# One plain feed-forward group instead of two, with the weight sums of gate and up on VectorE

## The chip, the cores and the metric

The kernel runs on one core of a Trainium2 chip. The metric is the device time of one launch in microseconds (us), the median of three runs. Engines are named as in the profile: PE is TensorE, which multiplies matrices (PEld is its weight load), DVE is VectorE, ACT is ScalarE, POOL is GpSimd, SP is SyncE, which issues nearly all DMAs.

## The reference

A decoder trunk of two layers over 1024 tokens of width 1024, in float32. Each layer mixes the tokens in four ways and adds the result to `x`; then comes the feed-forward part, which this change is about:

```python
D_FF = -(-8 * D_MODEL // (3 * 256)) * 256     # 2816
for l in range(DEPTH):                        # 2
    h = rmsnorm(x, attn_norm[l])
    proj = h @ w_in[l]
    ...                                       # latent attention, gated convolution, pooling, window attention
    x = x + mixed @ w_o[l]
    h2 = rmsnorm(x, ffn_norm[l])
    gate, up = jnp.split(h2 @ w_gate_up[l], 2, axis=-1)
    x = x + (jax.nn.silu(gate) * up) @ w_down[l]
return rmsnorm(x, final_norm)
```

## The kernel before

Activations lie with the features on the 128 partitions and the tokens along the row, in two halves of 512 tokens (`HALVES`). To keep float32 accuracy, each operand of a product is split into a high and a low part of type float32r: ScalarE casts (L283 or, with a gain, L286), VectorE subtracts (L284, L287). `mm3` (L272) then takes three matmuls for each pair of blocks: high x high, high x low, low x high.

The feed-forward's 2816 columns are worked through in 22 groups of 128 (`NFF`). A group computes gate and up for both halves of the tokens. There are two ways to do it. A *plain* group (`plain`, the first `NPL` = 2 groups of a layer) takes the weights as they are: for each half, gate and up are two products each (`product`) of four blocks, so eight products of 12 matmuls in all. Every other group treats gate/up and the two halves as a 2 x 2 matrix product in the Strassen-Winograd form, with seven products of 12 matmuls in place of eight. For that it needs sums and differences of both operands:

- of the activations, once a layer: `combine(j)` for j = 0 to 3 makes the blocks `hb[N1]`, `hb[N2]`, `hb[T3]`, `hb[T4]` from `hb[B11]`, `hb[B12]`, `hb[B21]`, `hb[B22]`, which `out_last` writes; VectorE and ScalarE do it (L1063, L1050, L1069, L1071 and the splits);
- of the weights, for each group: `GateUp.sums` (L1132 to L1134) and `GateUp.sum4` (L1154), four additions of 128x512 on GpSimd; `split1` to `split4` split the results;
- of the outputs: the products are added up in PSUM, where a copy by ScalarE (`snap`, L1176) and an addition by VectorE take intermediate values (L1188, L1502, L1514).

`gu_start` does a group's first two products, those with B11 and B21, which need no combined activations. `silu` (L1310) applies the activation on ScalarE and multiplies by the norm `r2` on GpSimd (L1312). `out_last` also adds up the squares for that norm (`ss2`, L324); `norm(u)` ends it. `combos(g)` makes, for each pair of groups, the same sums of the activations for the down projection and stores them to `ad`. The down projection has weight sums of its own: `dn_sums` loads blocks of `w_down`, adds them up on GpSimd in four operations of 128x256 (L161) and stores them to `qd`; the loop over the groups drives it with `next(sums)`, one block per group.

PSUM has eight banks of 128x512 in four tags (mm 2, s 3, t 2, pv 1); the tags of the seven-product groups rotate by the table `turns`. On-chip buffers are 47 slots of two halves, taken and returned first in, first out (`N_U`, `Slots`).

The order in which instructions are issued is not the written one. `order_engines` collects all instructions of the program, gives each group of instructions a place (its rank in the written order plus a shift from the table `MOVES`, by number of the group), and `arrange` simulates the engines with the costs in `length`; the ready instruction with the lowest place goes first. The order found is fixed with dependencies.

Of the kernel before, what the change touches and what calls it, by code (L numbers as in the profile page):

```python
# [25 lines left out]
NFF = DFF // P  # L26
# [15 lines left out]
NPL = 2  # L42
# [69 lines left out]
def trunk_kernel(ctx: ExitStack, tc: tile.TileContext, ins, out):  # L112
# [274 lines left out]
    for l in range(L):  # L387
# [731 lines left out]
        class GateUp:  # L1119
# [8 lines left out]
            def sums(self):  # L1128
                w1, w2 = self.raw
                q = self.q = F.pair()  # L1130
                a11, a22, a21 = F.ap(w1), F.ap(w1 + 1), F.ap(w2 + 1)
                pool.tensor_tensor(out=F.ap(q + 1), in0=a21, in1=a22, op=ALU.add)  # L1132
                pool.tensor_tensor(out=F.ap(q), in0=a21, in1=a11, op=ALU.add)
                pool.tensor_tensor(out=a21, in0=F.ap(q + 1), in1=a11, op=ALU.add)  # L1134
# [17 lines left out]
            def sum4(self):  # L1152
                q4 = F.ap(self.raw[1])
                pool.tensor_tensor(out=q4, in0=q4, in1=F.ap(self.raw[1] + 1), op=ALU.add)  # L1154
# [24 lines left out]
        def gu_start(w, between=None):  # L1179

            w.pa, pd = ps("aa"), ps("ad")
            product(w.pa, blocks(w.s1, 0), hb[B11])
            k1 = snap(w.pa)
            if between:
                between()
            product(pd, blocks(w.s2, 0), hb[B21])
            w.gate = tmp("tp")
            dve.tensor_tensor(out=w.gate, in0=pd, in1=k1, op=ALU.add)  # L1188
# [55 lines left out]
        for n in range(2):  # L1244
            R.free(kb_[1][n][1])
            R.free(va[2 + n][1])
        ma1 = norm_a(1)
        mix_values(*prev)
        for n in range(2):
            R.free(kb_[1][n][0])  # L1250
            R.free(va[n][1])
        ma0 = norm_a(0)
        out_some(len(parts))
# [3 lines left out]
        std = [GateUp(f) for f in range(2)]  # L1257
        std[0].split_plain()
# [4 lines left out]
        std[1].split_plain()  # L1263
# [4 lines left out]
        def plain(f, u):  # L1268

            w, b = std[f], ((B11, B21), (B12, B22))[u]  # L1270
            pg, pu = ps("wide"), ps("wide")
# [37 lines left out]
        def silu(g, r):  # L1309
            nonlocal last_silu  # L1310
            last_silu = act.activation(g, g, AF.Silu)  # L1311
            pool.tensor_tensor(out=g, in0=g, in1=r, op=ALU.mult)  # L1312
# [113 lines left out]
        w = GateUp(2)  # L1426
        plain(0, 0)
        combine(0)
        plain(1, 0)
        norm(0)  # L1430
        combine(1)
        plain_gates()
        plain(0, 1)
        norm(1)
        plain_silus()
        plain_gates()
        w.sums()
        combine(2)
        plain_acts()
        w.split1()  # L1440
        plain(1, 1)
        plain_silus()
        plain_gates()
        combine(3)
        w.split2()
        plain_acts()
# [3 lines left out]
        wn = GateUp(3)  # L1450
        w.split3()
        plain_silus()
        w.sum4()
        w.split4()
        plain_acts()
        for f in range(NPL, NFF):
            if wn:
                wn.sums()
            wnn = GateUp(f + 2) if f + 2 < NFF else None
            end = f == NFF - 1  # L1460
            gu_start(w, lambda: pending and second(*pending))
# [11 lines left out]
            if wn:  # L1473
# [5 lines left out]
            for i in w.s2:  # L1479
                R.free_pair(i)  # L1480
            k2 = snap(w.pa)
            if wn:
# [37 lines left out]
            neg_mul(F.ap(acts[f][0]), w.pa, gate)  # L1520
            if wn:
# [137 lines left out]
class Step:  # L1659
    __slots__ = ("ins", "eng", "rank", "before", "after", "tiles", "left", "ns", "tail", "ready", "sums", "bank", "onchip", "size", "start", "end", "table", "rows", "place")  # L1660

    def __init__(self, eng, rank):
# [4 lines left out]
        self.onchip = 0.0  # L1667
# [40 lines left out]
def length(eng, kind, i, ins, outs):  # L1708
    n = max(width(a) for a in ins + outs)
    ps = any(a.bass_ap.tensor.name.startswith("ps_") for a in ins)  # L1710
    if eng == "POOL":
        return 206 if kind == "InstMemset" else 1150 + 0.5 * n
# [19 lines left out]
def steps_of(tc):  # L1732
    steps, seen = [], {}
    table, runs = None, {"Silu": [], "Exp": []}
    for i in tc.nc.cur_bb.bb.instructions:
# [31 lines left out]
        else:  # L1767
            v.ns = length(eng, kind, i, ins, outs)
            if not any(a.bass_ap.tensor.name.startswith("ps_") for a in ins + outs):
                v.onchip = 0.7 if kind == "InstTensorScalarPtr" and len(ins) < 3 else 0.4  # L1770
# [39 lines left out]
def arrange(steps, rank=lambda v: v.rank):  # L1810
    queue, uses, freed, parked = {}, {}, {}, {}
# [21 lines left out]
    wire, pool_busy, last_fp32, table = 0.0, [], False, "Exp"  # L1833
# [5 lines left out]
    def takes(v, t):  # L1839
        for name in (x for x in v.tiles if x not in live):  # L1840
            tag = name.rsplit("_", 1)[0]
            if queue[tag][0] != name or not freed[tag] or freed[tag][0] + 40 > t:
# [3 lines left out]
    while any(now.values()) or any(later.values()):  # L1846
# [23 lines left out]
        for name in (x for x in v.tiles if x not in live):  # L1870
            tag = name.rsplit("_", 1)[0]
            if queue[tag][0] != name or not freed[tag]:
# [9 lines left out]
        for name in [x for x in v.tiles if x not in live]:  # L1882
            tag = name.rsplit("_", 1)[0]
            live.add(name)
            queue[tag].popleft()
            heapq.heappop(freed[tag])
# [17 lines left out]
        else:  # L1904
# [5 lines left out]
            if e == "DVE" and v.onchip:  # L1910
                ns += v.onchip * sum(max(0.0, min(b, t + ns) - max(a, t)) for a, b in pool_busy[-8:])
# [5 lines left out]
            if e == "POOL":  # L1917
                pool_busy.append((t, v.end))
# [6 lines left out]
        for name in v.tiles:  # L1925
            todo[name] -= 1
# [221 lines left out]
```

## Time and profile before

| | |
|---|---|
| median of 3 runs | 2062.74 us (2061.73 to 2062.99) |
| the profiled execution | 2061.72 us |
| its span, first to last instruction | 2059.9 us |
| granted TensorE clock | 0.998 |
| busy: PE, DVE, ACT, POOL | 2033.0, 1553.8, 979.5, 596.9 us |
| matmuls | 9418 |

In layer 0 `out_last` runs from about 366 us, the feed-forward's groups from about 388 to 820 us, the down projection to about 1040 us; layer 1 follows about 1010 us later. Busy times count every instruction from its start to its end, and instructions of one engine overlap at their edges, so a stretch can be all busy and still not be at the engine's best pace. In the timeline a row's first number is the start, the second the time from the first start to the last end of the merged instructions, and brackets hold the idle time before and what ended it.

### The profile page before, as it was taken

How to read it: one execution, taken by the hardware profiler on the slowest of the kernel's cores; microseconds unless marked ns; L12 is line 12 of the kernel's file. 1: busy time of each engine (PE TensorE's matmuls, PEld its weight loads, DVE VectorE, ACT ScalarE, POOL GpSimd, SP SyncE). 2: the span in 40 equal slices, each digit the busy share in tenths (PEclk: the TensorE clock that was granted, in tenths of full speed). 3: DMA queues.
4: the chain of work that ended last, by engine and by line, in shares of the span. 5: the costliest groups of instructions: out<-in, count | busy, mean ns of one | idle time of the engine just before them, and what ended most of it. 6: DMA issues, size and time to landing. Idle time of an engine off the chain costs nothing.

```text
span 2059.9 us, 26292 instructions
## 1 busy us (share of the span) xinstructions
PE 2033.0 (99%) x9418; PEld 1676.4 (81%) x9418; DVE 1553.8 (75%) x2430; ACT 979.5 (48%) x1722; POOL 596.9 (29%) x461
## 2 busy tenths in 40 slices
PE   8999999999999999999999999999999999999997
PEld 7887888878888888888888878878778888888887
DVE  7879988987776768655657898879877677686555
ACT  7447666653333334444443576666433333355332
POOL 0000000058776765100000000001787677640000
PEclk9999999999999999999999999999999999999999
DMA  5010222334444437866401102142444444498652
GB/s 181 34 58 24 79 88 86 138 121 168 170 156 167 166 138 257 313 221 204 152 33 44 47 21 91 64 144 81 160 168 163 153 166 153 145 333 278 197 177 86
DMA packets 148819, 289.76 MB, mean 141 GB/s; under 512 B 12608, under 2 KB 72000, under 8 KB 148688
## 3 DMA queue, kind: packets, MB, share of 16 engines
q1 hardware_dynamic: 148656, 288.03, 40.2%
q8 instruction: 74, 1.21, 0.2%
q14 instruction: 57, 0.47, 0.1%
q0 software_dynamic: 32, 0.04, 0.0%
HBM read 204.66 MB, written 83.36 MB: 140 GB/s over the span
## 4 chain that ended last, share of the span: by engine, by line
PE 89%; DVE 7%; DMA 1%; issue 1%; ACT 1%; POOL 1%; SPq 0%; DVEq 0%; ACTq 0%
PE ps_mm L272 35%; PE ps_s L272 26%; PE ps_t L272 10%; PE ps_pv L272 8%; DVE u L284 2%; PE ps_pv L962 2%; PE ps_t L950 1%; DVE u L287 1%; PE ps_s L896 1%; DVE u L324 1%; PE ps_t L336 1%; PE ps_s L898 1%; PE ps_s L897 1%; PE ps_pv L572 1%; DVE u L1099 1%
## 5 line engine op out<-in xcount | busy, mean ns | idle before, releaser
L272 PE MATMUL ps_mm<-u,u 128*128 128x512 f32 (+1 forms) x3394 | 848.8, 388 | 9.9 <-ACT u L286 7.1
L272 PEld LDWEIGHTS ps_mm<-u,u 128*128 128x128 f32 x3394 | 622.8, 188 | 136.2 <-ACT u L286 7.1
L272 PE MATMUL ps_s<-u,u 128*128 128x512 f32 x2648 | 649.4, 390 | 4.7 <-DVE u L284 3.6
L272 PEld LDWEIGHTS ps_s<-u,u 128*128 128x128 f32 x2648 | 496.8, 188 | 110.1 <-DVE u L284 4.4
L284 DVE TENSOR_TENSOR u<-u,u 128x1024 fp32r<-128x1024 f32 (+2 forms) x384 | 463.9, 1230 | 148.8 <-ACT u L283 129.3
L283 ACT CAST u<-u 128x1024 fp32r<-128x1024 f32 (+2 forms) x384 | 332.9, 888 | 464.9 <-PE ps_mm L272 178.4
L272 PE MATMUL ps_t<-u,u 128*128 128x512 f32 (+1 forms) x1146 | 274.4, 378 | 0.4 <-ACT u L283 0.4
L959 POOL MEMSET u<- 128x128 f32 x32 | 6.6, 230 | 847.8 <-PE ps_mm L272 637.8
L272 PEld LDWEIGHTS ps_t<-u,u 128*128 128x128 f32 x1146 | 206.3, 188 | 41.3 <-ACT u L283 0.8
L161 POOL TENSOR_TENSOR u<-u 128x256 f32<-128x256 f32 x176 | 196.8, 1118 | 73.2 <-DMA u<-in_w_dn 62.3
L1312 POOL TENSOR_TENSOR tp<-tp,u 128x512 f32<-128x512 f32 x88 | 147.1, 1672 | 209.6 <-ACT tp L1311 209.5
L272 PE MATMUL ps_pv<-u,u 128*128 128x512 f32 x744 | 184.7, 389 | 0.0
L272 PEld LDWEIGHTS ps_pv<-u,u 128*128 128x128 f32 x744 | 139.7, 188 | 29.0
L1311 ACT ACTIVATE tp<-tp 128x512 f32<-128x512 f32 x88 | 55.6, 632 | 134.1 <-DVE tp L348 133.4
L1132 POOL TENSOR_TENSOR u<-u,u 128x512 f32<-128x512 f32 x40 | 70.6, 1765 | 128.7 <-PE ps_s L272 55.5
L283 ACT CAST u<-ps_t 128x512 fp32r<-128x512 f32 (+4 forms) x136 | 64.8, 506 | 63.2 <-PE ps_t L950 38.9
L286 ACT ACTIVATE u<-u,par 128x512 fp32r<-128x512 f32 x100 | 69.3, 717 | 53.6 <-DVE u L1099 19.5
L284 DVE TENSOR_TENSOR u<-ps_t,u 128x512 fp32r<-128x512 f32 (+4 forms) x136 | 76.5, 583 | 17.8 <-ACT u L283 16.7
L287 DVE SCALAR_TENSOR_TENSOR u<-u,par,u 128x512 fp32r<-128x512 f32 x100 | 73.5, 757 | 7.5 <-ACT u L286 7.2
L348 DVE TENSOR_TENSOR tp<-tp,u 128x512 f32<-128x512 f32 x80 | 74.9, 936 | 1.1
L1514 DVE TENSOR_TENSOR tp<-ps_mm,tn 128x512 f32<-128x512 f32 x40 | 27.6, 690 | 63.4 <-PE ps_mm L272 63.4
L1154 POOL TENSOR_TENSOR u<-u 128x512 f32<-128x512 f32 x40 | 70.0, 1751 | 4.6 <-DVE u L284 4.6
(190 smaller groups left out, 2212.2 us busy)
## 6 DMA issues: line engine op xcount, KB each, us to landing
u<-in_w_gu SPq DMA_DIRECT2D x88, 512.0 KB, 4.3
ad<-u SPq DMA_DIRECT2D x154, 256.0 KB, 2.4
u<-ad SPq DMA_DIRECT2D x70, 512.0 KB, 5.8
u<-in_w_dn SPq DMA_DIRECT2D x68, 512.0 KB, 3.7
qd<-u SPq DMA_DIRECT2D x44, 512.0 KB, 2.9
u<-qd SPq DMA_DIRECT2D x32, 512.0 KB, 4.9
u<-in_w_in SPq DMA_DIRECT2D x30, 512.0 KB, 3.5
u<-in_xT SPq DMA_DIRECT2D x32, 256.0 KB, 5.0
```

The lines of the kernel that those rows point to most:

```text
L161: pool.tensor_tensor(out=o, in0=o, in1=u, op=ALU.add)
L272: pe.matmul(o, w, r, start=start and k == 0 and i == 0, stop=stop and k == n - 1 and i == 2, skip_group_check=again,)
L283: act.copy(hi, f)
L284: dve.tensor_tensor(out=lo, in0=f, in1=rd(hi), op=ALU.subtract)
L286: act.activation(hi, f, AF.Copy, scale=gain)
L287: dve.scalar_tensor_tensor(out=lo, in0=f, scalar=gain, in1=rd(hi), op0=ALU.mult, op1=ALU.subtract)
L348: dve.tensor_tensor(out=o, in0=a, in1=b, op=ALU.mult)
L962: pe.matmul(py[:, c0:], v_of(j, h), R.ap(s)[:, c0:], start=j == 0 and n == 0, stop=j == nj - 1 and n == 1,)
L1132: pool.tensor_tensor(out=F.ap(q + 1), in0=a21, in1=a22, op=ALU.add)
L1154: pool.tensor_tensor(out=q4, in0=q4, in1=F.ap(self.raw[1] + 1), op=ALU.add)
L1311: last_silu = act.activation(g, g, AF.Silu)
L1312: pool.tensor_tensor(out=g, in0=g, in1=r, op=ALU.mult)
```

## The change

- `NPL` is 1: group 1 of each layer becomes a group of seven products; group 0 stays plain.
- `sums`, `sum4` and the product in `silu` go to VectorE. The sums in `dn_sums` stay on GpSimd.
- The weights of groups 0 and 1 are loaded before `norm_a(1)` and around it; the splits of group 0, the sums of group 1 and its first two splits are written before `out_last`. Group 2 is loaded between the two calls of `out_last`.
- `gu_start` has an early form, which takes a bank of tag s and a slot for the gate; groups 1 and 2 are started in this form between the plain group's two halves and behind them, ahead of the loop.
- The plain group's products have fixed banks: mm and mm for the first half, t and s for the second.
- In the ordering, GpSimd's cost of an operation is 177 + 2.18 n ns for n columns in place of 1150 + 0.5 n; VectorE and GpSimd exclude each other when neither touches PSUM, in place of a surcharge on VectorE; a bank that an instruction takes ahead of its first writer is held for that one (`held_by`). `MOVES` is another table (490 entries in place of 430).

```diff
-NPL = 2
+NPL = 1
...
                 a11, a22, a21 = F.ap(w1), F.ap(w1 + 1), F.ap(w2 + 1)
-                pool.tensor_tensor(out=F.ap(q + 1), in0=a21, in1=a22, op=ALU.add)
-                pool.tensor_tensor(out=F.ap(q), in0=a21, in1=a11, op=ALU.add)
-                pool.tensor_tensor(out=a21, in0=F.ap(q + 1), in1=a11, op=ALU.add)
+                dve.tensor_tensor(out=F.ap(q + 1), in0=a21, in1=a22, op=ALU.add)
+                dve.tensor_tensor(out=F.ap(q), in0=a21, in1=a11, op=ALU.add)
+                dve.tensor_tensor(out=a21, in0=F.ap(q + 1), in1=a11, op=ALU.add)
...
-                pool.tensor_tensor(out=q4, in0=q4, in1=F.ap(self.raw[1] + 1), op=ALU.add)
+                dve.tensor_tensor(out=q4, in0=q4, in1=F.ap(self.raw[1] + 1), op=ALU.add)
...
-        def gu_start(w, between=None):
-
-            w.pa, pd = ps("aa"), ps("ad")
+        def gu_start(w, between=None, early=False):
+
+            w.pa, pd = ps("s" if early else "aa"), ps("ad")
...
-            w.gate = tmp("tp")
+            w.place = F.half() if early else None
+            w.gate = F.ap(w.place) if early else tmp("tp")
...
+        std = [GateUp(0)]
         ma1 = norm_a(1)
+        std[0].split_plain()
+        w = GateUp(1)
+        w.sums()
         mix_values(*prev)
...
+        w.split1()
         ma0 = norm_a(0)
+        w.split2()
         out_some(len(parts))
         out_last(HALVES[0], ma1)
...
-        std = [GateUp(f) for f in range(2)]
-        std[0].split_plain()
+        wn = GateUp(2)
         out_last(HALVES[1], ma0)
...
-        std[1].split_plain()
...
-            pg, pu = ps("wide"), ps("wide")
+            pg, pu = (ps("mm"), ps("mm")) if u == 0 else (ps("t"), ps("s"))
...
-            pool.tensor_tensor(out=g, in0=g, in1=r, op=ALU.mult)
+            dve.tensor_tensor(out=g, in0=g, in1=r, op=ALU.mult)
...
-        w = GateUp(2)
         plain(0, 0)
         combine(0)
-        plain(1, 0)
         norm(0)
+        gu_start(w, early=True)
         combine(1)
         plain_gates()
+        plain_silus()
+        plain_acts()
+        norm(1)
         plain(0, 1)
-        norm(1)
-        plain_silus()
-        plain_gates()
-        w.sums()
-        combine(2)
-        plain_acts()
-        w.split1()
-        plain(1, 1)
-        plain_silus()
-        plain_gates()
-        combine(3)
-        w.split2()
-        plain_acts()
...
-        wn = GateUp(3)
+        wn.sums()
+        wn.split1()
+        combine(2)
+        wn.split2()
+        gu_start(wn, early=True)
+        combine(3)
         w.split3()
-        plain_silus()
+        plain_gates()
         w.sum4()
         w.split4()
+        plain_silus()
         plain_acts()
         for f in range(NPL, NFF):
-            if wn:
+            soon = f == NPL
+            if wn and not soon:
                 wn.sums()
-            wnn = GateUp(f + 2) if f + 2 < NFF else None
+            wnn = GateUp(f + 2) if f + 2 < NFF and not soon else None
             end = f == NFF - 1
-            gu_start(w, lambda: pending and second(*pending))
+            if f > NPL + 1:
+                gu_start(w, lambda: pending and second(*pending))
+            elif pending:
+                second(*pending)
...
-        return 206 if kind == "InstMemset" else 1150 + 0.5 * n
+        return 206 if kind == "InstMemset" else 177 + 2.18 * n
...
-            if e == "DVE" and v.onchip:
-                ns += v.onchip * sum(max(0.0, min(b, t + ns) - max(a, t)) for a, b in pool_busy[-8:])
+            if e in held and v.onchip:
+                ns += max(0.0, held["POOL" if e == "DVE" else "DVE"] - 138 - t)
+                held[e] = t + ns
```

More of the change, by code (lines that the diff above doesn't have):

```diff
@@ L1472, in trunk_kernel @@
             mul_to(gate, gate, r2[0])
-            if wn:
+            if wn and not soon:
                 wn.split1()
@@ L1480, in trunk_kernel @@
                 R.free_pair(i)
+            if soon:
+                wnn = GateUp(f + 2)
             k2 = snap(w.pa)
-            if wn:
+            if wn and not soon:
                 wn.split2()
@@ L1520, in trunk_kernel @@
             neg_mul(F.ap(acts[f][0]), w.pa, gate)
+            if w.place is not None:
+                F.free(w.place)
             if wn:
@@ L1666, in __init__ @@
         self.sums = self.bank = None
-        self.onchip = 0.0
+        self.onchip = False
         self.table = self.rows = None
@@ L1769, in steps_of @@
             if not any(a.bass_ap.tensor.name.startswith("ps_") for a in ins + outs):
-                v.onchip = 0.7 if kind == "InstTensorScalarPtr" and len(ins) < 3 else 0.4
+                v.onchip = kind != "InstMemset"
             if ins:
@@ L1810, in arrange @@
 def arrange(steps, rank=lambda v: v.rank):
-    queue, uses, freed, parked = {}, {}, {}, {}
+    queue, uses, freed, parked, held_by = {}, {}, {}, {}, {}
     for v in steps:
@@ L1832, in arrange @@
     out = {e: [] for e in SIGNAL}
-    wire, pool_busy, last_fp32, table = 0.0, [], False, "Exp"
+    wire, last_fp32, table = 0.0, False, "Exp"
+    held = {"DVE": 0.0, "POOL": 0.0}
     before = {e: ((0, 0), 0.0) for e in SHIFT}
@@ L1841, in takes @@
             tag = name.rsplit("_", 1)[0]
-            if queue[tag][0] != name or not freed[tag] or freed[tag][0] + 40 > t:
+            if queue[tag][0] != name or tag in held_by or not freed[tag] or freed[tag][0] + 40 > t:
                 return False
@@ L1871, in arrange @@
             tag = name.rsplit("_", 1)[0]
-            if queue[tag][0] != name or not freed[tag]:
+            if queue[tag][0] != name or tag in held_by or not freed[tag]:
                 parked[tag].append((k, n, v))
@@ L1885, in arrange @@
             queue[tag].popleft()
+            if uses[name][0] is not v:
+                held_by[tag] = uses[name][0]
             heapq.heappop(freed[tag])
@@ L1916, in arrange @@
             free[e] = v.end - OVERLAP[e]
-            if e == "POOL":
-                pool_busy.append((t, v.end))
             if v.tail:
@@ L1925, in arrange @@
         for name in v.tiles:
+            tag = name.rsplit("_", 1)[0]
+            if held_by.get(tag) is v:
+                del held_by[tag]
+                for x in parked[tag]:
+                    heapq.heappush(later[x[2].eng], (v.start + 1, *x))
+                parked[tag] = []
             todo[name] -= 1
```

107 rows, old and new, of the table MOVES are left out of this document.

## The prediction

> **What bounds the kernel now.** I read the page first, for the shares.
>
> ```profile
> span 2059.9 us, 26292 instructions
> ...
> PE 2033.0 (99%) x9418; PEld 1676.4 (81%) x9418; DVE 1553.8 (75%) x2430; ACT 979.5 (48%) x1722; POOL 596.9 (29%) x461
> ```
>
> TensorE is never free for long, but its busy time is modelled, so its pace has to be read from starts. In the timeline of TensorE in layer 0's feed-forward, one product of 24 matmuls follows another:
>
> ```profile
> 427.43 5.60 PE L272 MATMUL ps_mm<-u,u 128*128 128x512 f32 x24
> 432.87 1.29 PE L272 MATMUL ps_s<-u,u 128*128 128x512 f32 x5
> ```
>
> From start to start that is 5.44 us for 24 matmuls, 226.7 ns each. Next, busy time by stretch (columns: PE, PEld, DVE, ACT, POOL with their instructions, granted clock, DMA share, GB/s):
>
> ```profile
> 500.00:800.00 300.00, 300.00 (x1325) 248.51 (x1324) 211.69 (x209) 103.41 (x144) 213.81 (x157) 1.00 0.47 163
> 420.00:460.00 40.00, 37.19 (x163) 30.01 (x162) 35.25 (x40) 19.14 (x30) 24.58 (x15) 1.00 0.46 152
> 1450.00:1510.00 60.00, 56.77 (x247) 45.52 (x246) 52.45 (x48) 23.21 (x34) 49.81 (x33) 1.00 0.48 163
> 370.00:420.00 50.00, 50.00 (x222) 41.17 (x221) 49.25 (x78) 35.54 (x58) 0.00 (x0) 1.00 0.24 90
> 340.00:370.00 30.00, 30.00 (x146) 24.31 (x145) 19.79 (x32) 15.83 (x27) 4.25 (x5) 1.00 0.43 154
> ```
>
> In the middle of the feed-forward, 1325 matmuls x 226.7 ns are 300.4 us of a stretch of 300: TensorE is at full pace and nothing else matters there. The second and third rows are the start of the feed-forward in layers 0 and 1; there matmuls are missing. The waits of TensorE in the timeline show where:
>
> ```profile
> 434.57 0.73 PE L272 MATMUL ps_t<-u,u 128*128 128x512 f32 x2 [0.41 <-ACT u L283]
> 452.31 0.50 PE L272 MATMUL ps_s<-u,u 128*128 128x512 f32 x1 [2.41 <-DVE u L284]
> 1455.72 2.56 PE L272 MATMUL ps_mm<-u,u 128*128 128x512 f32 x10 [0.92 <-DVE u L284]
> 1488.70 2.11 PE L272 MATMUL ps_s<-u,u 128*128 128x512 f32 x8 [1.14 <-DVE te L1502]
> 1504.23 2.11 PE L272 MATMUL ps_s<-u,u 128*128 128x512 f32 x8 [1.17 <-DVE u L284]
> ```
>
> These add to 2.8 us in layer 0 and 3.2 us in layer 1, nearly all waits for VectorE. So the time is the number of matmuls at 226.7 ns, plus what VectorE makes TensorE wait at the start of each feed-forward.
>
> **Part 1: fewer matmuls.** A plain group takes, for each half of the tokens, four products of 4 blocks x 3 matmuls: 2 x 4 x 4 x 3 = 96. A group with seven products takes 7 x 4 x 3 = 84. One group per layer changes its kind, so 12 matmuls a layer and 24 in all go: 24 x 0.2267 = 5.4 us. They lie on the path, since TensorE has no slack. This is the only sure term.
>
> **Part 2: the steady groups.** Six operations of 128x512 per group go from GpSimd to VectorE: the three sums of L1132 to L1134, the fourth of L1154, and two products at L1312. The groups of instructions give the prices (after the bar: busy us, mean ns of one, then idle before):
>
> ```profile
> L1132 POOL TENSOR_TENSOR u<-u,u 128x512 f32<-128x512 f32 x40 | 70.6, 1765 | 128.7 <-PE ps_s L272 55.5 <-ACT tn L318 46.0 <-DVE u L284 23.5
> L161 POOL TENSOR_TENSOR u<-u 128x256 f32<-128x256 f32 x176 | 196.8, 1118 | 73.2 <-DMA u<-in_w_dn 62.3 <-DVE u L1305 1.3
> L348 DVE TENSOR_TENSOR tp<-tp,u 128x512 f32<-128x512 f32 x80 | 74.9, 936 | 1.1
> L1305 DVE SCALAR_TENSOR_TENSOR u<-te,tp 128x512 f32<-128x512 f32 x40 | 45.6, 1140 | 20.4 <-POOL tp L1312 20.4
> L1514 DVE TENSOR_TENSOR tp<-ps_mm,tn 128x512 f32<-128x512 f32 x40 | 27.6, 690 | 63.4 <-PE ps_mm L272 63.4
> ```
>
> VectorE takes 690 ns for 512 columns when one input is in PSUM (L1514), and 936 to 1140 ns on average when both are in on-chip buffers (L348, L1305): the surplus is waiting for GpSimd. A group of seven products lasts 84 x 0.2267 = 19.0 us. From the row of 500 to 800 us, VectorE is busy 211.7 / 300 x 19.0 = 13.4 us of it, and GpSimd 13.6 us. Six more at 0.69 us make VectorE 17.5 us if its waiting stays as it is. But GpSimd keeps only the four operations of L161, 4 x 1.118 = 4.5 us of its 13.6, so waiting falls: by the surplus of the quoted lines alone 2 x 0.25 + 0.45, or about 1 us a group. I take 16.5 us, between 15.5 (more of the waiting gone) and 17.5, under 19.0 at either end. The cost is nothing, and the cover is some 2 us of VectorE's idle time per group. Every second group also runs the four operations of `combos`, 1.4 us above the mean: 18.9 at the worst, still just below.
>
> What the remaining L161 operations can cost VectorE is bounded by a row for one of them alone:
>
> ```profile
> 458.99 0.73 POOL L161 TENSOR_TENSOR u<-u 128x256 f32<-128x256 f32 x1
> ```
>
> So 2.9 us a group if each holds VectorE for its bare length, 4.5 us if for its mean one. [...]
>
> **Part 3: the start of the feed-forward.** This is the open term. The first product that needs all four blocks of `hb[N2]` used to come behind 4 x 48 + 24 = 216 matmuls (49.0 us); now behind 96 for the plain group and 24 each for two started groups, 144 (32.6 us). The four `combine` calls, VectorE's work, are due 16.3 us earlier. The first of the plain matmuls, the split of a pair of blocks by itself (1.2 us), and the last split of N2 now:
>
> ```profile
> 388.34 5.60 PE L272 MATMUL ps_mm<-u,u 128*128 128x512 f32 x24
> ...
> 395.30 1.21 DVE L284 TENSOR_TENSOR u<-u,u 128x1024 fp32r<-128x1024 f32 x1
> ...
> 438.14 1.40 DVE L284 TENSOR_TENSOR u<-tp,u 128x512 fp32r<-128x512 f32 x1 [0.30 <-ACT u L283]
> ```
>
> Adding about 1 us for the norms' own matmuls, TensorE will want N2 near 388.3 + 32.6 + 1 = 422 us; today it is complete at about 439. VectorE has to gain 17 us in a stretch in which it was busy 49.25 of 50 us (370 to 420). It is freed of the second plain group's splits (2 x 1.2), gates and products (4 x 0.69), and of the first seven-product group's splits (2 x 1.2) and sums, which are now asked for before 370, where the row of 340 to 370 leaves it 10 us idle: 7.6 us. Between 420 and 460 it idles for 4.8 us by the row above, and single pairs of splits last longer than 2 x 0.69 us because GpSimd works beside them, which will have nothing to do there:
>
> ```profile
> 427.63 2.34 DVE L284 TENSOR_TENSOR u<-tp,u 128x512 fp32r<-128x512 f32 x2
> ```
>
> I count 6 us for both up to 440, an estimate from these rows. Against this stand the second started group's sums and splits (3 x 0.69 + 2 x 1.2), two gate sums and two products (4 x 0.69): 7.2 us. Net 6.4 us of 17. The rest must come from order. The sums of squares of L324 can wait, because only the two norms need them, and all products up to there fit in the eight PSUM banks of the tags mm, s, t and pv:
>
> ```profile
> L324 DVE TENSOR_TENSOR u<-u,tn 128x512 f32<-128x512 f32 (+1 forms) x66 | 42.5, 653 | 2.6 <-ACT u L313 1.4 <-ACT tn L318 1.0
> ```
>
> Sixteen per layer at 653 ns are 10.4 us. So the stall lies between 0 and 10.6 us a layer, against 2.8 and 3.2 now: from 3 us better to 7.6 worse, per layer. I take no change, 3 us a layer, which means that some 7.5 of the 10.4 us are put back: the written order has `norm(1)` behind `combine(1)` and the acts of the first half, but `norm(0)` early, so not all of it can go.
>
> **Part 4: loads and the order.** The median time from issue to landing of the weights' loads is the last number here:
>
> ```profile
> u<-in_w_gu SPq DMA_DIRECT2D x88, 512.0 KB, 4.3
> ```
>
> These loads move earlier on SP's queue, past the reads of `out_last`. With tens of us between load and split, 4.3 us are hidden; without that cover they would show once a layer. The table of shifts is replaced for the whole program. Outside the feed-forward's start TensorE's waits are these (total, times, longest):
>
> ```profile
> PE ps_mm L272 <- ACT u L286: 7.1, 1, 7.1
> PE ps_mm L272 <- ACT u L215: 1.9, 2, 1.0
> PE ps_s L336 <- DVE u L320: 1.4, 1, 1.4
> ```
>
> The 7.1 us is the program's first load and stays. About 3 us could go, and as much could come: I take 0, keeping 3 us to either side. The additional block of `dn_sums` in the loop (one per group, 21 groups less the last) is covered as in part 2.
>
> **The sum.** 2061.7 us for the profiled execution (span 2059.9 and 1.8 around it) less 5.4 is 2056.3. That execution lies 1.0 us below the median of the runs, 2062.74, so I say 2057.3 us, with 2052 to 2061 as this case's own range. About 0.2% (4.1 us) is what a measurement of this kernel can tell from no change, so faster means below 2058.6.
>
> **The rivals.** *The start gives the gain back.* If only half of L324's work is put back, 5.2 us, the stall is 5.4 us a layer, 10.8 against 6.0 now: 4.8 us of the gain are eaten and the time is 2062.1, no change. For it: VectorE's 49.25 of 50 us. Against it: ten idle microseconds just before.
>
> *VectorE becomes the bound at the start: slower.* Same place, but with nothing put back: 10.6 us a layer, 21.2 against 6.0, so 15.2 - 5.4 = 9.8 us slower, 2072.5. It decides from a stall of 7.8 us a layer on, where the gain and another 4.1 us are eaten. [...]
>
> *VectorE becomes the bound in the steady groups.* At 18.9 of 19.0 us a group with `combos` has no room; if such a group slips by 1 us, ten a layer cost 20 us: 2072. Against it: the waiting that falls away with GpSimd's work.
>
> That the change does not do what it says is no case here, since the number of matmuls follows from the loops.
>
> *The start gets better too.* All waits there vanish: 5.4 + 6.0 = 11.4 us, 2051.3.
>
> **The chances.** The forecast has 0.47 (0.39 of it below 2058.6), the better start 0.11, the gain given back 0.2, the two slower ones 0.15 and 0.07. That makes faster 0.5, same 0.28, slower 0.22. The range from 2051 to 2069 leaves out the worst of the slower cases, and a little at the other end.
>
> **What would show it.** Right: 24 matmuls fewer on the page (9394); VectorE at 82 to 92% between 500 and 800 us with TensorE still at 222 matmuls per 50 us; GpSimd near 200 us in all; waits of TensorE on L284 or L1502 at the start of each feed-forward of about 3 us. Wrong: TensorE waiting for VectorE anywhere in the steady stretch, or a wait over 5 us before a product with N2 or N1; and new waits in the attention stages would show that the order, not the work, decided.

## The result, and the profile after

The changed kernel takes 2055.61 us (median; 2054.87 to 2058.24) against 2062.74, 7.1 us less. The ratio over all runs of both is 0.9968 (0.32% less), with a 95% interval of 0.9958 to 0.9979. The forecast was 2057.3 us, with faster as the likeliest case. The profiled execution of after took 2055.69 us, and its span is 2053.8, 6.1 us shorter than that of before; the other 1.0 us is the distance of before's profiled execution from its own median.

The page of after, its span and busy times:

```profile
span 2053.8 us, 26189 instructions
...
PE 2030.9 (99%) x9394; PEld 1670.3 (81%) x9394; DVE 1616.5 (79%) x2696; ACT 991.6 (48%) x1738; POOL 203.5 (10%) x213
```

24 matmuls are gone, GpSimd has lost two thirds of its time, and VectorE, with 266 more instructions, is busy for only 63 us more. The same five stretches as before (columns PE, PEld, DVE, ACT, POOL, granted clock, DMA share, GB/s):

```profile
500.00:800.00 300.00, 300.00 (x1323) 247.61 (x1322) 235.77 (x301) 106.50 (x147) 67.24 (x60) 1.00 0.47 163
420.00:460.00 40.00, 39.27 (x172) 31.71 (x171) 38.41 (x54) 20.64 (x32) 9.19 (x8) 1.00 0.54 184
1450.00:1510.00 60.00, 59.22 (x261) 48.29 (x260) 55.32 (x73) 22.71 (x31) 20.51 (x19) 1.00 0.62 211
370.00:420.00 50.00, 49.90 (x220) 40.69 (x219) 49.47 (x79) 37.81 (x62) 0.00 (x0) 1.00 0.26 97
340.00:370.00 30.00, 30.00 (x143) 24.22 (x143) 27.62 (x47) 17.45 (x31) 0.38 (x2) 1.00 0.31 99
```

The middle of the feed-forward still runs at full pace, 1323 matmuls in 300 us. In the two starts the counts have risen from 163 to 172 and from 247 to 261. Between 340 and 370 us VectorE is busy 27.6 us where it was 19.8: its idle time ahead of `out_last` is used up. TensorE's waits at the two starts, in its timeline:

```profile
426.57 0.74 PE L272 MATMUL ps_mm<-u,u 128*128 128x512 f32 x2 [0.73 <-ACT u L283]
1403.50 1.39 PE L272 MATMUL ps_s<-u,u 128*128 128x512 f32 x5 [0.38 <-ACT u L283]
1441.43 0.74 PE L272 MATMUL ps_mm<-u,u 128*128 128x512 f32 x2 [0.96 <-ACT u L283]
1469.92 0.73 PE L272 MATMUL ps_s<-u,u 128*128 128x512 f32 x2 [0.78 <-ACT u L283]
```

They add to 2.85 us, where before had 6.05. So the span's 6.1 us are 5.4 of matmuls (24 x 226.7 ns) and 3.2 of waits at the starts, less about 2.5 us that came back in the rest of the program, whose order is another. No single row holds them, but the starts of the matmuls in the two traces show where they lie. Against a pace of 226.7 ns for 512 columns, and in proportion for fewer (an estimate), TensorE falls behind by 67.7 us in before and by 67.4 in after. At the two starts (388 to 480 and 1360 to 1520 us) after loses 3.4 us less. It loses 0.5 more ahead of them in layer 0 (before 388 us), 1.0 more in layer 1's attention (1040 to 1360), and 0.9 and 0.5 more in small pieces behind the starts (480 to 1040 and from 1520 on). In these two executions the gain at the starts is thus nearly lost again, and the difference of the spans is close to the 24 matmuls alone.

VectorE's groups with both inputs in on-chip buffers, below GpSimd's own (mean ns of one after the busy time; L1310 in the numbering of after is L1305 of before):

```profile
L161 POOL TENSOR_TENSOR u<-u 128x256 f32<-128x256 f32 x176 | 196.0, 1116 | 759.0 <-DMA u<-in_w_dn 502.3 <-DVE tp L348 63.3 <-DVE u L1310 35.1
L348 DVE TENSOR_TENSOR tp<-tp,u 128x512 f32<-128x512 f32 x80 | 60.1, 751 | 1.6
L1310 DVE SCALAR_TENSOR_TENSOR u<-te,tp 128x512 f32<-128x512 f32 x42 | 41.5, 987 | 0.1
L1132 DVE TENSOR_TENSOR u<-u,u 128x512 f32<-128x512 f32 x42 | 29.9, 712 | 6.0 <-PE ps_s L272 4.9 <-DMA u<-in_w_gu 0.2
```

L348 went from 936 to 751 ns and the product at L1310 from 1140 to 987. A sum that cost GpSimd 1765 ns costs VectorE 712.

### The profile page after: what moved, and what is told of

It reads as the page before. It is cut to its first block, busy times and chain, and to the rows that moved or that the text cites. A ratio compares the mean times of both kernels' runs of the same rounds, so it can differ in the third digit from the quotient of the medians.

```text
span 2053.8 us, 26189 instructions
## 1 busy us (share of the span) xinstructions
PE 2030.9 (99%) x9394; PEld 1670.3 (81%) x9394; DVE 1616.5 (79%) x2696; ACT 991.6 (48%) x1738; POOL 203.5 (10%) x213
## 4 chain that ended last, share of the span: by engine, by line
PE 72%; DVE 2%; ACT 2%; DMA 1%; POOL 0%; issue 0%; SPq 0%; DVEq 0%; ACTq 0%; POOLq 0%
PE ps_s L272 25%; PE ps_mm L272 25%; PE ps_t L272 10%; PE ps_pv L272 8%; PE ps_pv L962 1%; PE ps_t L950 1%; DMA ad<-u 1%; ACT u L283 0%; PE ps_s L896 0%; POOL u L161 0%; PE ps_t L336 0%; PE ps_s L897 0%; PE ps_s L898 0%; PE ps_s L511 0%; PE ps_mm L770 0%
## 5 line engine op out<-in xcount | busy, mean ns | idle before, releaser
L272 PE MATMUL ps_mm<-u,u 128*128 128x512 f32 (+1 forms) x3426 | 868.2, 390 | 2.6 <-ACT u L283 1.7
L272 PE MATMUL ps_s<-u,u 128*128 128x512 f32 x2676 | 662.3, 391 | 8.0 <-ACT u L286 6.8
L283 ACT CAST u<-u 128x1024 fp32r<-128x1024 f32 (+2 forms) x388 | 336.4, 889 | 388.8 <-PE ps_s L272 83.8
L284 DVE TENSOR_TENSOR u<-u,u 128x1024 fp32r<-128x1024 f32 (+2 forms) x388 | 403.5, 1060 | 148.5 <-ACT u L283 124.0
L272 PE MATMUL ps_t<-u,u 128*128 128x512 f32 (+1 forms) x1118 | 267.2, 378 | 0.0
L272 PE MATMUL ps_pv<-u,u 128*128 128x512 f32 x696 | 171.4, 390 | 0.0
L272 PEld LDWEIGHTS ps_pv<-u,u 128*128 128x128 f32 x696 | 130.5, 188 | 27.3 <-ACT tn L1176 0.2
L283 ACT CAST u<-ps_t 128x512 fp32r<-128x512 f32 (+4 forms) x136 | 64.7, 506 | 46.4 <-PE ps_t L950 29.4
L284 DVE TENSOR_TENSOR u<-ps_t,u 128x512 fp32r<-128x512 f32 (+4 forms) x136 | 76.3, 581 | 9.1 <-ACT u L283 8.5
L1317 DVE TENSOR_TENSOR tp<-tp,u 128x512 f32<-128x512 f32 x84 | 63.2, 753 | 20.3 <-ACT tp L1316 19.8
L1176 ACT COPY tn<-ps_s 128x512 f32<-128x512 f32 x66 | 38.4, 583 | 78.8 <-PE ps_s L272 78.7
L216 DVE TENSOR_TENSOR u<-u,u 128x1024 fp32r<-128x1024 f32 (+1 forms) x46 | 51.8, 1128 | 26.0 <-PE ps_t L272 12.3
L318 ACT ACTIVATE tn<-u 128x512 f32<-128x512 f32 (+1 forms) x93 | 52.7, 590 | 36.4 <-DVE u L1575 31.6
L348 DVE TENSOR_TENSOR tp<-tp,u 128x512 f32<-128x512 f32 x80 | 60.1, 751 | 1.6
```

The source lines that it names most:

```text
L216: dve.tensor_tensor(out=lo[:, :n], in0=raw[:, :n], in1=rd(hi[:, :n]), op=ALU.subtract)
L272: pe.matmul(o, w, r, start=start and k == 0 and i == 0, stop=stop and k == n - 1 and i == 2, skip_group_check=again,)
L283: act.copy(hi, f)
L284: dve.tensor_tensor(out=lo, in0=f, in1=rd(hi), op=ALU.subtract)
L318: act.activation(q, f, AF.Square)
L348: dve.tensor_tensor(out=o, in0=a, in1=b, op=ALU.mult)
```

## The experiments

Each kernel was timed in runs that alternate with runs of the kernel before; ratios are to that kernel.

**The two halves of the change, one at a time.** First the engine move undone (here, in the next kernel and in `product_on_gpsimd`, the product keeps its number in the table of shifts, so that the table's other numbers still fit):

```diff
 # after.py, in sums, sum4 and silu
-dve.tensor_tensor(...)
+pool.tensor_tensor(...)
```

> The change with its engine move undone: one plain group, but sums, sum4 and the product in silu on GpSimd, as before. Theory (the gain is the 24 matmuls, and the move to VectorE is needed only because the start of the feed-forward has become tighter): the 9394 matmuls stay, the steady stretch stays at 222 matmuls per 50 us, and the start stalls 2 to 6 us more in the two layers together, so 2058 to 2062. Rival 1 (the move does nothing for the time): 2055 to 2057. Rival 2 (the move is the gain, the matmuls are not): about 2062, with waits of TensorE in the steady stretch too.

Measured: 2078.44 us, ratio 1.0071 (1.0059 to 1.0084), 15 us slower than before. The theory had the direction but not the size, and both rivals' times are out; that the move carries the gain, the thought behind rival 2, is not. TensorE's timeline in the start of layer 0, then the stretch of 50 us there and the steady one:

```profile
423.18 0.50 PE L272 MATMUL ps_s<-u,u 128*128 128x512 f32 x1 [0.28 <-ACT u L283]
423.90 1.53 PE L272 MATMUL ps_s<-u,u 128*128 128x512 f32 x4 [0.23 <-DVE u L284]
427.50 4.63 PE L272 MATMUL ps_t<-u,u 128*128 128x512 f32 x10 [2.07 <-DVE u L284]
...
465.30 1.22 PE L272 MATMUL ps_t<-u,u 128*128 128x512 f32 x2 [4.07 <-ACT u L283]
```

```profile
420.00:470.00 50.00, 42.55 (x160) 32.44 (x159) 42.89 (x46) 22.55 (x34) 29.62 (x21) 0.87 0.42 143
500.00:800.00 300.00, 300.00 (x1324) 248.03 (x1323) 216.28 (x208) 101.87 (x143) 223.91 (x162) 1.00 0.47 158
```

The steady stretch is untouched, 1324 matmuls. The loss lies in the start: 160 matmuls in 50 us, where full pace is 220. That is 13.7 us, while the waits in the same stretch add to about 7.5 (its PE column). Of the rest, 4.0 us go with the granted clock, 0.87 here: twenty matmuls stand 427 ns apart instead of 227, eleven behind the wait of 2.07 us and nine behind that of 4.07. Layer 1's start loses too: between 1450 and 1510 us it has 219 matmuls at a clock of 0.97, where after has 261. The table of shifts in this kernel is the one made for the sums on VectorE; no run has one made for GpSimd, so a part of the loss may be the order's.

Then the engine move alone, with two plain groups:

```diff
 # before.py, in sums, sum4 and silu
-pool.tensor_tensor(...)
+dve.tensor_tensor(...)
```

> The kernel before with the engine move alone: two plain groups, sums, sum4 and the product in silu on VectorE. Theory: 9418 matmuls at the same pace, the steady stretch unchanged, at best some of the 6 us of waits at the starts less, so 2059 to 2063. Rival (the move is the gain): 2056 to 2058.

Measured: 2058.2 us, ratio 0.9973 (0.9963 to 0.9984), 4.7 us faster than before. That lies between the two forecasts, 0.8 us below the theory's 2059 and 0.2 above the rival's 2058. TensorE's waits at the starts in that kernel:

```profile
456.59 2.56 PE L272 MATMUL ps_s<-u,u 128*128 128x512 f32 x10 [0.34 <-DVE u L284]
460.21 0.73 PE L272 MATMUL ps_t<-u,u 128*128 128x512 f32 x2 [0.60 <-ACT u L283]
1471.28 2.58 PE L272 MATMUL ps_s<-u,u 128*128 128x512 f32 x10 [1.46 <-DVE u L284]
```

2.4 us against 6.05: the move alone removes 3.6 us of what the starts waited. Put together (the lower row has the early loads and starts, the planner's new costs and the new table with it):

| ratio to before | sums on GpSimd | sums on VectorE |
|---|---|---|
| two plain groups | 1 | 0.9973 |
| one plain group | 1.0071 | 0.9968 |

One plain group costs 15 us with the sums on GpSimd, and gains little over 1 us by the ratios with the sums on VectorE (intervals overlap; 3.5 us by the spans, 2057.3 and 2053.8). The parts do not add: the move carries most of the gain, and it is what lets the other part be kept. That the other part gains anything on top of it is not shown beyond the intervals.

**The price of matmuls.** The first product of the plain group's first half is taken twice:

```diff
+            if u == 0:
+                product(pg, blocks(w.s1, 0), hb[b[0]], True, True)
             product(pg, blocks(w.s1, 0), hb[b[0]], True, False)
```

> The kernel after, with the first 12 matmuls of the plain group's first half done twice (the first time is thrown away): 24 more in all, 9418 as before. Theory (TensorE is the path and each matmul costs 226.7 ns): 5.4 us more, 2060 to 2062. Rival (the start waits for VectorE anyway, so more matmuls there fill waits): 2056 to 2058, with the waits at the start gone.

Measured: 2063.41 us, ratio 1.0002 (0.9993 to 1.0011), span 2060.8. Against after's span that is 7.0 us for 24 matmuls, 5.4 of them by their pace; by the medians it is 7.8. The theory's mechanism holds, though the time is 1.4 us above its 2062, and the rival is out: waits did not swallow the matmuls.

**Only the product back.** Of what went to VectorE, the product in `silu` returns to GpSimd and the sums stay:

```diff
-            dve.tensor_tensor(out=g, in0=g, in1=r, op=ALU.mult)
+            pool.tensor_tensor(out=g, in0=g, in1=r, op=ALU.mult)
```

> The kernel after with the product in silu alone back on GpSimd; the sums of gate and up weights stay on VectorE. In sums_on_gpsimd both are back and it takes 2078.4 us, with all the loss at the starts and half of it in a slower granted clock after waits of 2 us and more. Theory (the four sums a group, 4 x 1.3 us of GpSimd alone and the hold on VectorE, made the starts late): 2056 to 2060, no wait over 2 us at the starts, no episode of matmuls at 427 ns there. Rival (the product, in the chain from the gate to the act, made them late): over 2067.

Measured: 2062.89 us, ratio 0.9999 (0.999 to 1.0008): between the two, so neither. Given the sums on VectorE, the product is worth some 7 of the 23 us that separate `sums_on_gpsimd` from after, the sums the remaining 16. The main waits at the starts, in a profiled execution that was the slowest of its eleven (2067.31 us):

```profile
425.52 3.88 PE L272 MATMUL ps_t<-u,u 128*128 128x512 f32 x10 [2.07 <-DVE u L284]
461.36 0.73 PE L272 MATMUL ps_s<-u,u 128*128 128x512 f32 x2 [2.02 <-ACT u L283]
...
1444.33 0.97 PE L272 MATMUL ps_s<-u,u 128*128 128x512 f32 x3 [1.10 <-ACT u L283]
1452.18 0.73 PE L272 MATMUL ps_mm<-u,u 128*128 128x512 f32 x2 [1.66 <-ACT u L283]
```

The theory wanted no wait over 2 us and no matmuls at 427 ns; both are there.

**The last work of GpSimd moved too.**

```diff
 # dn_sums
-                pool.tensor_tensor(out=o, in0=o, in1=u, op=ALU.add)
+                dve.tensor_tensor(out=o, in0=o, in1=u, op=ALU.add)
```

> The kernel after with the sums of the down projection's weights on VectorE too, so that GpSimd does nothing in the feed-forward. Theory (steady groups have room on VectorE either way): VectorE has 4 more operations of 256 columns a group but never waits for GpSimd, no change, 2054 to 2057. Rival (GpSimd's hold on VectorE costs TensorE time now): 2050 to 2053. A second rival (VectorE is full): over 2058, with waits of TensorE in the steady stretch.

Measured: 2057.93 us, ratio 0.9972 (0.996 to 0.9983), no difference from after beyond the intervals, though 0.9 us above the theory's 2057. TensorE does not wait in the steady stretch (1323 matmuls between 500 and 800 us), so the second rival's sign is absent. What GpSimd still does costs nothing that can be seen where it is, and nothing is won by moving it.

**How much room VectorE has.** The first sum of each group is repeated:

```diff
+                for _ in range(4):          # 8 in vector_plus8
+                    dve.tensor_tensor(out=F.ap(q + 1), in0=a21, in1=a22, op=ALU.add)
                 dve.tensor_tensor(out=F.ap(q + 1), in0=a21, in1=a22, op=ALU.add)
```

> The kernel after with the first sum of each seven-product group done five times instead of once: 4 more operations of 128x512 on VectorE, 4 x 0.69 = 2.8 us a group of 19.0 us. VectorE was busy 235.8 of 300 us, 15.0 us a group. Theory (4 us of room): 17.8 us a group, TensorE keeps its pace in the steady stretch, the starts lose up to 2 us a layer, 2055 to 2060. Rival (VectorE is nearly the bound, every operation more shows): 21 groups x 2 layers x 1 us or more, over 2090.

> The same with 8 more operations, 5.5 us a group, so 20.5 us of busy time for 19.0 us of matmuls; starts of neighbouring operations overlap by 0.08 us, which makes the demand 18.5 to 20.5. Theory: VectorE becomes the bound, 0 to 1.5 us a group more, 42 groups with 40 that do these sums: 2060 to 2120. Rival (order and not room is what counts): already past 2100 with 4 more.

Measured: 2088.26 us (ratio 1.0126, 1.0111 to 1.014) and 2211.57 us (1.0712, 1.0686 to 1.0737). That is 33 and 156 us over after, both more than the theories allowed; with four it is close to the rival's 2090. Where, for four more operations and then for eight:

```profile
420.00:470.00 50.00, 45.44 (x184) 34.68 (x183) 45.56 (x64) 23.61 (x35) 11.94 (x10) 0.97 0.43 137
500.00:600.00 100.00, 93.72 (x393) 76.32 (x394) 81.43 (x109) 32.77 (x45) 26.63 (x20) 0.95 0.46 152
650.00:800.00 150.00, 150.00 (x663) 124.21 (x662) 125.82 (x182) 51.00 (x72) 45.74 (x31) 1.00 0.45 151
```

```profile
600.00:800.00 200.00, 176.56 (x741) 143.58 (x740) 165.45 (x239) 56.73 (x79) 67.69 (x36) 0.94 0.39 128
```

With four, the steady groups do have the room: 663 matmuls in 150 us is full pace. It is the start that has none, and its backlog takes until about 650 us to clear. With eight, TensorE does 741 matmuls in 200 us where 882 fit, although VectorE is busy only 83% of that time, and the granted clock is 0.94. So the waits come before the engine is full. The fixed order may be why; no run separates that.

**Order.** Without the table's shifts in the starts alone:

```diff
-        v.place = v.rank + MOVES.get(groups[k], 0)
+        v.place = v.rank + (0 if 2600 <= v.rank < 3500 or 9580 <= v.rank < 10480 else MOVES.get(groups[k], 0))
```

> The kernel after without the table's shifts in the start of each feed-forward alone, from the first load of gate and up weights to some groups into the loop; the rest of the table stays. Theory (the start was saved by order): waits of TensorE there grow by 3 to 10 us in all, 2059 to 2066. Rival (the written order with its early starts does it): 2055 to 2057.

Measured: 2065.25 us, ratio 1.0014 (1.0005 to 1.0023): the theory, 9.6 us over after. Without any shift, in both kernels:

```diff
-        v.place = v.rank + MOVES.get(groups[k], 0)
+        v.place = v.rank + 0
```

> The kernel after with every shift of its table at zero, so that the written order and the planner's costs alone decide. Theory (the order table is worth as much as the change, in both kernels alike): 15 to 40 us slower than after, 2070 to 2095, most of it in the attention stages and the starts. Rival (the new costs of the planner do the work without the table): under 2062.

> The kernel before with every shift at zero. Theory: slower by about as much as after_no_shifts is against after, so that the difference of the two without a table is again 3 to 10 us. Rival (the change is only a better table): the two are within 2 us without their tables, or the kernel before is then the faster one.

Measured: 2080.72 us (ratio 1.0081, 1.0067 to 1.0094) and 2087.58 us (1.0121, 1.0105 to 1.0136). The tables are worth about 25 us in each kernel, and the change is worth 0.40% without them and 0.32% with them. So it isn't a better table that makes the result. The planner's costs differ between these two kernels as well, and no run changes them alone; `two_plain_sums_vector`, which has the costs and the table of before, shows only that the engine move needs neither.

With the shifts of the kernel before in layer 1's attention:

```diff
 MOVES = {
-    # groups 2100 to 3284: after's shifts
+    # groups 2100 to 3284: before's shifts of groups 2121 to 3305
```

> The kernel after with the shifts of the kernel before in layer 1's attention stages (those groups are the same in both, their numbers differ by 21). In the profiles those stages lose 1 us more in after than in before. Theory (these stages are independent of the start that follows): 1 us less, 2054 to 2055.5. Rival (the start was prepared in them: VectorE's and the loads' work ahead of out_last): 1 to 5 us more.

Measured: 2062.26 us, ratio 0.9996 (0.9987 to 1.0004), some 6 us over after: the rival's direction, and somewhat more than its 1 to 5 us. A wait stands in the start that follows:

```profile
1446.56 0.73 PE L272 MATMUL ps_s<-u,u 128*128 128x512 f32 x2 [2.96 <-ACT u L283]
```

The last `combine` of that layer begins at 1443.31 us, 4.9 us later than in after (1438.43), although the first begins only 0.5 later. So what is fixed in the attention stages reaches into the start that follows; by which operations was not traced.

**One that did not do what it was for.** The early work on group 1 was to be delayed:

```diff
+        if v.ins[0].name in LATE:        # splits of group 0, sums and first splits of group 1
+            v.place += 250
```

> The kernel after, with the splits of group 0 and the sums and first splits of group 1 given places 250 later, so that they come behind out_last instead of in the idle time of VectorE before it. Theory (the start holds because VectorE's idle 10 us ahead of out_last are filled now): some 7 us of VectorE's work come back into the full stretch, the starts stall 3 to 7 us more a layer, 2061 to 2070. Rival (the start is paced by the combine calls alone, whenever these splits run): under 2058.

Measured: 2057.44 us, ratio 0.9977 (0.9968 to 0.9986). That is in the rival's range (under 2058), but it proves nothing, for the sums stayed where they were, at 343.8 us:

```profile
343.81 0.69 DVE L1137 TENSOR_TENSOR u<-u,u 128x512 f32<-128x512 f32 x1
```

A place is only a priority; the planner gives an idle engine whatever is ready. Whether the use of the idle time ahead of `out_last` is what holds the start is thus shown by no run, only by the two profiles.

## Why the prediction was right, and where its reasons were not

**Part 1, the matmuls**, was right in count (9394) and close in price: 24 matmuls more cost 7.0 us in `extra_matmuls`. But I let this term stand for the whole gain, as "the only sure term". It is not a gain by itself: `sums_on_gpsimd` has the 9394 matmuls and is 15 us slower than before. And that the total came within 1.7 us of the forecast is in part luck: I had no change in the waits at the starts and none elsewhere, and measured were 3.2 us less and about 2.5 more, which nearly cancel.

**Part 2, the steady groups**, was right in the verdict and off in size. I took 16.5 us of VectorE per group, between 15.5 and 17.5; 235.77 / 300 x 19.0 is 14.9, below my lower bound, and VectorE's share of that stretch is 79% where I had 82 to 92%. The term that was mis-sized is the waiting for GpSimd: it fell by some 2.6 us a group instead of 1 (17.5 less 14.9), for the splits were longer beside GpSimd's work too, which I had not counted. Their mean in before and in after:

```profile
L284 DVE TENSOR_TENSOR u<-u,u 128x1024 fp32r<-128x1024 f32 (+2 forms) x384 | 463.9, 1230 | 148.8 <-ACT u L283 129.3 <-PE ps_s L272 6.3 <-PE ps_pv L272 4.3
...
L284 DVE TENSOR_TENSOR u<-u,u 128x1024 fp32r<-128x1024 f32 (+2 forms) x388 | 403.5, 1060 | 148.5 <-ACT u L283 124.0 <-issue 5.4 <-PE ps_t L272 4.7
```

In before, 138 of the 254 splits of 128x1024 from on-chip buffers on that line overlap an operation of GpSimd and take 1683 ns on average, the other 116 take 1221; of L348's 80 operations, 46 overlap one and take 1122 ns, the other 34 take 685. Of the 40 at L1514, with one input in PSUM, 38 overlap one and take 690. What the sums left on GpSimd could cost VectorE, 2.9 or 4.5 us a group, was my estimate. In after, 14 of L348's 80 operations overlap one of them and take 1042 ns, the other 66 take 690, and `dn_sums_vector`, which has none of these sums on GpSimd, is no faster (2057.93 us). That VectorE and GpSimd exclude each other when neither touches PSUM is the planner's assumption; these numbers have its direction.

There is room for four operations more in these groups, as `vector_plus4` showed after 650 us.

**Part 3, the start**, is the step that failed. I forecast unchanged waits of about 3 us a layer; they were 0.7 and 2.1, and all four are put down to ScalarE's cast (L283), where I had named VectorE's L284 and L1502. I gave 6 us, by estimate, to what VectorE would win from idling and from GpSimd's absence up to 440 us, and looked for the rest in the sums of squares (L324) going behind `combine`. They did not go: in after's timeline the last of them starts at 395.42, ahead of the first `combine` at 397.28 (and there are 12 per layer on that line, not 16, so the term was 7.8 us and not 10.4). What made the difference is that the whole of VectorE's work came forward. Its first addition of `out_last` (L1099) and the last `combine`, its beginning (L1063) and the splits that end with N2's (L284), in after:

```profile
362.64 1.28 DVE L1099 TENSOR_TENSOR u<-u,ps_s 128x512 f32<-128x512 f32 x2
...
424.18 0.74 DVE L1063 SCALAR_TENSOR_TENSOR tp<-u,par,te 128x512 f32<-128x512 f32 x1
...
426.04 1.89 DVE L284 TENSOR_TENSOR u<-tp,u 128x512 fp32r<-128x512 f32 x3
```

and the first addition and the same `combine` in before:

```profile
370.01 0.68 DVE L1099 TENSOR_TENSOR u<-u,ps_t 128x512 f32<-128x512 f32 x1
...
434.77 0.73 DVE L1063 SCALAR_TENSOR_TENSOR tp<-u,par,te 128x512 f32<-128x512 f32 x1
```

So the first addition comes 7.4 us sooner and the last `combine` 10.6. That `combine` begins at 427.36 us in `sums_on_gpsimd` and at 435.19 in `two_plain_sums_vector`: 7.4 of the 10.6 us are there with one plain group and the new order alone, and none with the engine move alone. Nor did VectorE have to gain the 17 us that I asked for. The plain group's matmuls and those of the two started groups, 144, are done at about 422.5, as I had put it, while the last split of N2 ends at about 428, 11.6 us sooner than in before and not 17. TensorE ran 15 other matmuls in between and waited 0.73 us.

That the sums and products on GpSimd were a large part of the start's trouble is shown: `two_plain_sums_vector` removes 3.6 of the 6.05 us of waits by the move alone. Whether they hurt by holding VectorE up (L348 at 936 ns against 751) or by their own length (1765 ns against 712) no run separates. My price for the moved operations, "nothing", was their price in the steady groups; at the start the move is a gain, which I had as the case that the start gets better too, at 0.11.

**The rivals.** That VectorE becomes the bound at the start did not happen, but the place was the right one: `sums_on_gpsimd`, `product_on_gpsimd`, `vector_plus4` and `no_shifts_start` all lost time there. The other slower rival, the steady groups, needed eight more operations to appear; its price was also added up wrongly, for 20 us more and 5.4 less than 2062.7 is 2077 and not 2072.

**More work for a busy VectorE.** Between 420 and 460 us of before, where GpSimd's operations ran beside it, VectorE was busy 35.25 of 40 us, and giving it six operations a group more made the start faster (2.4 us of waits at the two starts against 6.05, in `two_plain_sums_vector`). In the fullest stretch, 49.25 of 50 us, GpSimd had no work (0.00), so no run tests there whether moving work off VectorE would help.

What stays open: how the 7.1 us divide between the engine move and the matmuls (1.0 us for the latter by the ratios, 3.5 by the spans), how much of the latter is owed to the early loads and the planner's new costs, and which changes of order gave the 2.5 us back.

## What to carry to other kernels

Where an operation takes longer beside another engine's work (L348 in before: 1122 ns where it overlaps an operation of GpSimd, 685 where it does not), that work is not free, even if the other engine looks idle: read the mean time of the same operation with and without the other engine beside it, and count that surplus at the place where the fast engine has no slack. Price an engine move and the change that it makes possible in all four combinations; here the one was worth 5 us alone and the other cost 15 us alone. And look for the tight place at the seams between stages: four more operations a group were free in the middle of the feed-forward and cost 33 us through its start and the backlog behind it.

## What was not expected of the hardware

Some waits of TensorE cost more than their length in these runs. In `sums_on_gpsimd`, after waits of 0.28, 0.23 and 2.07 us within five, the matmuls stand 427 ns apart for some 5 us before they return to 227, and nine matmuls behind the wait of 4.07 us do the same; the granted clock between 420 and 470 us is 0.87. In `product_on_gpsimd` a wait of 2.07 us with no other near it brought seven matmuls at that pace (the ten from 425.52 us take 3.68 us, 2.27 at full pace), and a wait of 1.66 us, 8 us behind one of 1.10, brought some more (the ten from 1453.53 us take 3.98). But in the same run the 36 matmuls behind a wait of 2.02 us stand 232 ns apart on average, and so do the 25 behind a single wait of 2.41 us in before. So the length of a wait alone does not decide (2.07 and 1.66 us brought such matmuls, 2.02 and 2.41 did not); what does, no run shows.
